# Cached attention in pairs of steps, with the transposes of its exponentials set apart

## The chip, the core and the metric

The program runs on one core of a Trainium2 chip. The metric is the device time of one launch in microseconds (us), as the median of several runs. Beside it stands one profiled execution, whose trace gives every number below that is not a run's time. The engines are TensorE (PE: matrix products; PEld: its weight loads), VectorE (DVE), ScalarE (ACT), GpSimd (POOL) and SyncE (SP, which here mostly issues loads). Each works through its own queue in order.

## The reference, cut to what matters

One step of a decoder layer over 512 prompt rows and 64 sample rows (8 sequences of 8 new positions). A projection gives queries, keys, values, forget-gate logits and the input of a convolution. Eight heads of 128 attend; the sample rows attend to 2048 cached positions, which a page table finds, and to the new ones. After it come the output projection, an MLP, a gated embedding and norms. The part that the change touches:

```python
def fox_attention_sample(q, k_new, v_new, logf_new, k_past, v_past, logf_past):
    ...
    s_past = jnp.einsum('bqhd,bkhd->bhqk', q, k_past).astype(jnp.float32) * scale
    s_past = s_past + cn[..., :, None] + r_past[..., None, :]
    ...
    p = jax.nn.softmax(jnp.concatenate([s_past, s_new], axis=-1), axis=-1).astype(v_new.dtype)
    return (jnp.einsum('bhqk,bkhd->bqhd', p[..., :P], v_past)
            + jnp.einsum('bhqk,bkhd->bqhd', p[..., P:], v_new))
```

## The kernel before

The program has two phases. The first, up to about 745 us, holds the input projection, both attentions and the convolution; the second the output projection, the MLP, the gate and the last norm. The order of work on every engine is written out by hand with Python generators: each `yield` ends a piece of work, and a loop decides whose piece comes next.

**The projection** sets the beat. A tile of 128 output columns (`gemm_tile`) takes four weight chunks of 256 KB; after each half of a chunk, 12 matmuls of 288 columns into bank U on L513, it yields. This piece is called a half tile here. Weights come through `WStream`: ACT issues the load (wraw, L117, five tiles in turn) and copies it to a rounded form (whi, L128), DVE makes the rest (wlo, L134), up to two chunks ahead of PE.

**Between two half tiles** `run` calls `half` once: first `flush_later`, which issues what was put off for a half tile (mostly exponentials, so that ACT does not wait in line for DVE), then one piece of the convolution, of the prompt heads (`att`) and of side work, and last, by a credit that grows by `DEC_RATE` (0.2275 to 0.2775), a step of cached attention, about one in four half tiles.

**Cached attention** (`decode`) has 68 steps. Four steps make a group: the 512 columns of one bank, for four sequences and four heads. A step n computes

- scores (up to n = 63), into bank D (`D_()`): at a group's first step one product that brings in the forget bias (R), then 8 products of 32 query columns with two k tiles. After the fourth step DVE adds a bias and takes the maximum (tile dp, in the source p); the exponential is put off to `later`, for ACT.
- values (from n = 4), for the group before, into bank O (`O_()`): 16 products of a 32-column piece of PT with two v tiles. PT holds the transposed exponentials of a group. After the fourth step DVE merges O into the running sum (`merge`).

The trace shows a product of these as two rows, 16 and 32 in a step. At the first step of a group, ahead of its scores, PE transposes the four blocks of the last group's exponentials into bank T (`T_()`, L869), and ACT copies them to PT in two pieces (L871). Bank T is also the prompt heads': their transposed exponentials, v_s (L798) and the end of each head, amt (L820), go through it. Each of the banks S, T, O and D has one buffer.

**The cache loads** (`kv_load`, L847) stand in SP's queue. A tile of keys or values is 512 KB in two loads; keys have five tiles, values four. A step's calls of `load` send, in this order, the second k tile and two v tiles for two steps later, and the first k tile for three steps later. A load waits for the products that read the tile's last content, and for the eighth load before it on the hardware queues, SP's and ACT's together, since eight completion semaphores are given out in turn.

Of the kernel before, what the change touches and what calls it, by code (L numbers as in the profile page):

```python
# [12 lines left out]
AF = mybir.ActivationFunctionType  # L13
# [134 lines left out]
class Kern:  # L148
# [111 lines left out]
    def phase1(self):  # L260
        tc, nc, a = self.tc, self.nc, self.a
# [108 lines left out]
        D = {"credit": 0.0, "dec": None, "mid": None, "rate": 0.0}  # L370

        def step(q):
            while q:
                try:
                    next(q[0])
                    return True
                except StopIteration:
                    q.popleft()
            return False

        def half():

            self.flush_later()
            if D["dec"] is None:
                step(att)
                step(fq)
                return
            step(side)
            step(att)
            step(pq)  # L390
            D["credit"] += D["rate"]
            if D["credit"] >= 1.0:
                D["credit"] -= 1.0
                if next(D["dec"], self) is self and D["mid"] is None:
                    des.close()
                    D["mid"] = mes.enter_context(tc.tile_pool(name="mid", bufs=2, reuse_waits="tile"))
                    self.ple_loads(D["mid"])
                    pq.append(self.ple_ahead(D["mid"]))
                    side.append(self.finish(1, D_, O_))

        def run(gen):
            for _ in gen:
                half()
# [41 lines left out]
        dec = D["dec"] = self.decode()  # L445
        next(dec)

        for n, (kind, i) in enumerate(order):
# [12 lines left out]
            if kind == "q":  # L461
                t = hd.tile([128, NR], F32, name="q", tag="q", bufs=2)
# [15 lines left out]
        n = 0  # L478
# [251 lines left out]

    def flush_later(self):

        for fn in self.later:
            fn()
        self.later = []


    def prompt_head(self, h, hb):
# [112 lines left out]
    def decode(self):  # L851


        nc, sm = self.nc, self.sm
        V = nc.vector.tensor_tensor
        tiles, load = self.kv, self.kv_load
        s = o = mu = p = None
        al, ls = {}, {}
        one = lambda name: sm.tile([128, 1], F32, name=name, tag=name)
        for n in range(68):  # L860
            if n == 0:
                load(0, 5)
                yield
            sc, w = n // 4, n % 4
            G, c = sc // 4, sc % 4
            if n >= 4 and w == 0:
                t = self.T_()
                for i in range(4):
                    nc.tensor.transpose(t[:, i * 128:i * 128 + 128], p[:, i * 128:i * 128 + 128], self.ident)  # L869
                for i, m in ((0, 128), (128, 512)):  # L870
                    nc.scalar.activation(self.PT[:, i:m], t[:, i:m], AF.Copy)  # L871
            if n < 64:
                if w == 0:
                    s = self.D_()
                    nc.tensor.matmul(s, self.selU[:, G, :], self.R[:, c * 512:c * 512 + 512], start=True, stop=False)
                for i in range(2):
                    kt = tiles[0][2 * n + i]
                    for h in range(4):
                        nc.tensor.matmul(s[32 * h:32 * h + 32, i * 256:i * 256 + 256].rearrange("p (a b) -> p a b", a=2),  # L879
                                         self.q_of(G // 2 * 4 + h, G % 2 * 4 + w), kt[:, :, h, :],  # L880
                                         start=False, stop=(w == 3 and i == 1))
                if w == 3:
                    p = self.kvp[1].tile([128, 512], F32, name="dp", tag="dp")
                    mx = one("dmx")
                    nc.vector.tensor_scalar(p, s, self.cns[:, G:G + 1], None, ALU.add, ALU.max, accum_out=mx)
                    new = self.mlu[:, 0, G:G + 1]
                    if c == 0:
                        nc.vector.tensor_copy(new, mx)
                        ls[sc] = self.mlu[:, 1, G:G + 1]
                    else:  # L890
                        al[sc], ls[sc] = one("dal"), one("dls")
                        V(mx, mx, new, ALU.max)
                        V(al[sc], new, mx, ALU.subtract)
                        nc.vector.tensor_copy(new, mx)
                    nm = one("dnm")
                    nc.vector.tensor_scalar(nm, mx, -1.0, None, ALU.mult)

                    def late(p=p, nm=nm, l=ls[sc], d=al.get(sc)):
                        nc.scalar.activation(p, p, AF.Exp, bias=nm, accum_out=l)
                        if d is not None:  # L900
                            nc.scalar.activation(d, d, AF.Exp)
                    self.later.append(late)
                load(0, 2 * n + 6)
            if n >= 4:
                m = n - 4
                if w == 0:
                    o = self.O_()
                for r in range(4):
                    for h in range(4):
                        nc.tensor.matmul(o[32 * h:32 * h + 32, r * 128:r * 128 + 128], self.PT[:, w * 128 + h * 32:w * 128 + h * 32 + 32],  # L910
                                         tiles[1][2 * m + r // 2][:, r % 2, h, :], start=(w == 0 and r == 0), stop=(w == 3 and r == 3))
                if w == 3:
                    self.merge(m // 16, m // 4 % 4, o, al.pop(m // 4, None), ls.pop(m // 4))
            load(1, 2 * n - 2)
            load(0, 2 * n + 7)
            yield

    def merge(self, G, c, o, al, l):

# [881 lines left out]
class Beside:  # L1801
# [41 lines left out]
    def wait(self, t, dt):  # L1843
        self.now = t
        self.credit = min(max(self.credit, -3.0) + dt, dt)
# [173 lines left out]
```

## Time and profile before

| what | value |
|---|---|
| median of 3 runs | 2682.98 us (2680.68 to 2690.61) |
| the profiled execution's own time | 2673.58 us |
| its span, first to last instruction | 2671.5 us |
| granted TensorE clock | 0.997 |
| PE / DVE / ACT / POOL busy, share of the span | 98% / 77% / 44% / 20% |
| score products (L879), count and mean | 1024, 385 ns |
| value products (L910), count and mean | 2048, 273 ns |
| transposes of exponentials (L869), count and mean | 64, 274 ns |

The profile's page gives busy time by engine, the span in 40 slices of 67 us, the chain of work that ended last, and groups of instructions. Matmuls overlap on PE, so a sum of their durations is more than the time that they take; what a burst costs is read from starts, in the view in order of time. There, a row with a count merges like instructions that follow each other, with the start of the first and the time to the end of the last.

### The profile page before, as it was taken

What the parts mean: (1) busy time and instruction counts of PE and PEld (TensorE: products, weight loads), DVE (VectorE), ACT (ScalarE), POOL (GpSimd) and SP (SyncE); (2) the same over time, 40 slices, a digit from 0 to 9 for tenths busy, and PEclk for the clock granted to TensorE, in tenths of its full rate; (3) what the DMA queues carried; (4) which work ended last, traced back from release to release, by engine and by line L of the source; (5) the groups of instructions that cost most, each with busy time, mean ns of one, the idle gap of its engine ahead of it and who ended that gap; (6) DMA issues with size and microseconds to landing.
All of it is one profiled execution on the core that took longest, in us unless ns stands there. A gap on an engine that the chain in (4) does not pass through costs nothing.

```text
span 2671.5 us, 56560 instructions
## 1 busy us (share of the span) xinstructions
PE 2631.2 (98%) x21937; PEld 2555.2 (96%) x21937; DVE 2050.0 (77%) x3575; ACT 1164.8 (44%) x1722; POOL 521.0 (20%) x919
## 2 busy tenths in 40 slices
PE   9999999999999999999999999999999999999997
PEld 8899999888999999999999999999999999999997
DVE  6577777656564348888998888899888888898676
ACT  5222223335453335444544444545444444444554
POOL 2288786711010000000100000110000000000110
PEclk9999999999999999999999999999999999999998
DMA  6598999899764554444444444767565666656675
GB/s 206 172 305 292 300 297 303 291 319 319 270 200 148 164 195 157 156 143 157 168 163 143 144 145 143 253 184 219 154 199 137 174 173 175 174 187 217 196 241 169
DMA packets 241327, 544.39 MB, mean 204 GB/s; under 512 B 25921, under 2 KB 26946, under 8 KB 241058
## 3 DMA queue, kind: packets, MB, share of 16 engines
q1 hardware_dynamic: 172562, 330.95, 38.6%
q0 software_dynamic: 34960, 148.86, 17.7%
q10 hardware_dynamic: 33536, 60.96, 7.1%
q8 instruction: 172, 2.82, 0.4%
q14 instruction: 97, 0.79, 0.1%
HBM read 445.60 MB, written 95.09 MB: 202 GB/s over the span
## 4 chain that ended last, share of the span: by engine, by line
PE 85%; issue 5%; DVE 5%; DMA 3%; ACT 1%; POOL 0%; SPq 0%; ACTq 0%; DVEq 0%; POOLq 0%
PE U L513 20%; PE P L1661 17%; PE P L1662 16%; PE P L1663 16%; PE P L1731 2%; PE P L1730 2%; PE P L1729 2%; PE D L879 2%; PE O L910 2%; DVE w2l L157 1%; DMA wraw<-in_w_main 1%; DMA xs<-dl 1%; PE S L753 1%; PE S L773 1%; DMA w2r<-in_w_down 0%
## 5 line engine op out<-in xcount | busy, mean ns | idle before, releaser
L1661 PE MATMUL P<-xs,w2h 128*128 128x288 f32 x3584 | 1061.5, 296 | 5.2 <-DVE c L1778 4.7
L1662 PE MATMUL P<-xs,w2h 128*128 128x288 f32 x3584 | 1056.7, 295 | 3.2 <-DVE xs L157 2.8
L1663 PE MATMUL P<-xs,w2l 128*128 128x288 f32 x3584 | 1051.5, 293 | 0.6 <-DVE w2l L157 0.5
L154 ACT ACTIVATE w2h<-w2r 128x896 fp32r<-128x896 f32 (+1 forms) x632 | 558.9, 890 | 758.9 <-PE P L1662 439.4
L157 DVE TENSOR_TENSOR w2l<-w2r,w2h 128x896 fp32r<-128x896 f32 (+1 forms) x632 | 637.9, 1012 | 197.5 <-ACT w2h L154 191.7
L1661 PEld LDWEIGHTS P<-xs,w2h 128*128 128x128 f32 x3584 | 672.7, 188 | 9.6 <-DVE c L1778 6.7
L1662 PEld LDWEIGHTS P<-xs,w2h 128*128 128x128 f32 x3584 | 675.0, 188 | 5.1 <-DVE xs L157 4.3
L1663 PEld LDWEIGHTS P<-xs,w2l 128*128 128x128 f32 x3584 | 675.0, 188 | 1.5 <-DVE w2l L157 1.5
L513 PE MATMUL U<-xh,whi 128*128 128x288 f32 x1792 | 399.3, 304 | 0.4 <-ACT xh L154 0.4
L513 PE MATMUL U<-xl,whi 128*128 128x288 f32 x1792 | 383.1, 295 | 1.8 <-DVE xl L348 0.9
L513 PE MATMUL U<-xh,wlo 128*128 128x288 f32 x1792 | 383.5, 296 | 0.0
L513 PEld LDWEIGHTS U<-xh,whi 128*128 128x128 f32 x1792 | 286.8, 189 | 19.0 <-issue 16.3
L128 ACT ACTIVATE whi<-wraw 128x512 fp32r<-128x512 f32 x224 | 140.9, 630 | 354.6 <-PE U L513 323.8
L513 PEld LDWEIGHTS U<-xl,whi 128*128 128x128 f32 x1792 | 288.0, 188 | 2.8 <-DVE xl L348 1.4
L513 PEld LDWEIGHTS U<-xh,wlo 128*128 128x128 f32 x1792 | 287.9, 188 | 0.0
L134 DVE TENSOR_TENSOR wlo<-wraw,whi 128x512 fp32r<-128x512 f32 x224 | 159.8, 714 | 118.3 <-ACT whi L128 117.9
L1059 DVE SCALAR_TENSOR_TENSOR y<-ue,cv,y 128x512 f32<-128x512 f32 x240 | 183.7, 765 | 5.3
L1884 DVE TENSOR_TENSOR w2r<-w2r 128x512 f32<-128x512 f32 (+1 forms) x273 | 177.9, 652 | 10.9 <-DMA w2r<-in_w_down 10.7
L1060 POOL TENSOR_SCALAR cvt<-us,cv 128x64 f32<-128x64 f32 x240 | 165.8, 691 | 22.3
L1731 PE MATMUL P<-xs,w2l 128*128 128x288 f32 x512 | 151.0, 295 | 1.1 <-DVE w2l L157 1.0
L1730 PE MATMUL P<-xs,w2h 128*128 128x288 f32 x512 | 150.9, 295 | 0.8 <-DVE xs L1570 0.8
L1729 PE MATMUL P<-xs,w2h 128*128 128x288 f32 x512 | 151.3, 295 | 0.0
(413 smaller groups left out, 2795.2 us busy)
## 6 DMA issues: line engine op xcount, KB each, us to landing
k<-in_cache_kv SPq DMA_DIRECT2D x256, 256.0 KB, 4.3
v<-in_cache_kv SPq DMA_DIRECT2D x256, 256.0 KB, 4.5
w2r<-in_w_up SPq DMA_DIRECT2D x127, 512.0 KB, 3.9
w2r<-in_w_down SPq DMA_DIRECT2D x112, 512.0 KB, 4.3
wraw<-in_w_main ACTq DMA_DIRECT2D x156, 256.0 KB, 4.7
xs<-di POOLq DMA_DIRECT2D x32, 1008.0 KB, 6.2
w2r<-in_w_gate SPq DMA_DIRECT2D x60, 512.0 KB, 4.8
x<-c POOLq DMA_DIRECT2D x48, 576.0 KB, 5.8
```

Of the source, the lines that this page charges most:

```text
L154: self.nc.scalar.activation(out, in_, AF.Copy, **kw)
L157: self.nc.vector.tensor_tensor(out, in_, f(hi), ALU.subtract)
L513: self.nc.tensor.matmul(u[:, r, :HR], w, x[:, r * HR:(r + 1) * HR], start=first and n == 0, stop=last and n == 2)
L1059: nc.vector.scalar_tensor_tensor(y, ue[:, j:j + NPR], w, y, ALU.mult, ALU.add)
L1060: nc.gpsimd.tensor_scalar(t, us[:, :, j:j + 8], w, None, ALU.mult)
L1661: nc.tensor.matmul(o, hi[:, ia, :], s.hi[:, ib, :], start=(i == 0), stop=False)
L1662: nc.tensor.matmul(o, hi[:, ia, :], s.lo[:, ib, :], start=False, stop=False)
L1663: nc.tensor.matmul(o, lo[:, ia, :], s.hi[:, ib, :], start=False, stop=(i == n - 1))
L1729: nc.tensor.matmul(o, hi[:, ia, :], s.hi[:, kh, rows], start=first and kh == 0, stop=False)
L1730: nc.tensor.matmul(o, hi[:, ia, :], s.lo[:, kh, rows], start=False, stop=False)
L1731: nc.tensor.matmul(o, lo[:, ia, :], s.hi[:, kh, rows], start=False, stop=last and kh == 1)
L1884: lambda: V(w[:, :, 4:6, :], w[:, :, 0:1, :].broadcast_to([128, m, 2, 128]), w[:, :, 1:3, :], ALU.add),
```

## The change

Three things are different.

1. `half` waits until the credit is 2 and then takes two steps of cached attention one after the other. The rate is the same, so two steps stand in one burst every seven to nine half tiles. As step numbers go in pairs from 0, a group's steps are two bursts: first and second, third and fourth. The last step no longer yields, so that the second call of the last pair reports the end.
2. The transposes leave the first step of the next group. They are a function `turn` that is put into `later` by a new helper `wait`, which hands it on through three flushes: the exponential is issued one half tile after the group's last scores, the transposes three half tiles after that. They go to bank D, the score bank, and ACT copies all 512 columns to PT in one instruction. A loop at a group's first step flushes until its transposes are done, if they aren't yet.
3. `flush_later` takes the list away before it calls its entries, so that an entry may put off another.

```diff
-            if D["credit"] >= 1.0:
-                D["credit"] -= 1.0
-                if next(D["dec"], self) is self and D["mid"] is None:
+            if D["credit"] >= 2.0:
+                D["credit"] -= 2.0
+                if [next(D["dec"], self) for _ in range(2)][1] is self and D["mid"] is None:
...
-        for fn in self.later:
+        fns, self.later = self.later, []
+        for fn in fns:
             fn()
-        self.later = []
+
+    def wait(self, k, fn):
+
+        self.later.append((lambda: self.wait(k - 1, fn)) if k else fn)
...
-            if n >= 4 and w == 0:
-                t = self.T_()
-                for i in range(4):
-                    nc.tensor.transpose(t[:, i * 128:i * 128 + 128], p[:, i * 128:i * 128 + 128], self.ident)
-                for i, m in ((0, 128), (128, 512)):
-                    nc.scalar.activation(self.PT[:, i:m], t[:, i:m], AF.Copy)
+            while n >= 4 and w == 0 and turned[0] < sc:
+                self.flush_later()
...
-                    def late(p=p, nm=nm, l=ls[sc], d=al.get(sc)):
+                    def turn(p=p):
+                        t = self.D_()
+                        for i in range(4):
+                            nc.tensor.transpose(t[:, i * 128:i * 128 + 128], p[:, i * 128:i * 128 + 128], self.ident)
+                        nc.scalar.activation(self.PT, t, AF.Copy)
+                        turned[0] += 1
+
+                    def late(p=p, nm=nm, l=ls[sc], d=al.get(sc), turn=turn):
                         nc.scalar.activation(p, p, AF.Exp, bias=nm, accum_out=l)
                         if d is not None:
                             nc.scalar.activation(d, d, AF.Exp)
+                        self.wait(2, turn)
...
-            yield
+            if n < 67:
+                yield
```

The next two pieces are the difference on PE, at the start of the third group (- before, + changed). At the place where a burst with the transposes stood, half a pair after the second group's last scores:

```order
 L513 MATMUL U<-xh_209,wlo 128x288 x2
-L869 MATMUL T<-ident,dp 128x128 x4
-L875 MATMUL D<-R,selU 128x512
-L879 MATMUL D<-k,q_s 32x256 x8
-L910 MATMUL O<-v,PT 32x128 x16
+L902 MATMUL D<-ident,dp 128x128 x4
 L513 MATMUL U<-xh_195,whi 128x288 x2
```

The transposes stay there alone, in bank D, and the step has moved down. Next on PE, where the group's second step stood:

```order
 L513 MATMUL U<-xh_201,wlo 128x288 x2
-L879 MATMUL D<-k,q_s 32x256 x8
-L910 MATMUL O<-v,PT 32x128 x16
+L876 MATMUL D<-R,selU 128x512
+L880 MATMUL D<-k,q_s 32x256 x8
+L919 MATMUL O<-v,PT 32x128 x16
+L880 MATMUL D<-k,q_s 32x256 x8
+L919 MATMUL O<-v,PT 32x128 x16
 L513 MATMUL U<-xh_203,whi 128x288 x2
```

Both steps now stand there, without projection between them. On ACT the copies to PT keep their place among the weight chunks. Before:

```order
L899 ACTIVATE dp,dls<-dp,dnm 128x512
L901 ACTIVATE dal<-dal 128x1
L117 DMA wraw<-in_w_main 128x512
L128 ACTIVATE whi<-wraw 128x512
L117 DMA wraw<-in_w_main 128x512
L128 ACTIVATE whi<-wraw 128x512
L871 ACTIVATE PT<-T 128x128
L871 ACTIVATE PT<-T 128x384
```

Changed:

```order
L907 ACTIVATE dp,dls<-dp,dnm 128x512
L909 ACTIVATE dal<-dal 128x1
L117 DMA wraw<-in_w_main 128x512
L128 ACTIVATE whi<-wraw 128x512
L117 DMA wraw<-in_w_main 128x512
L128 ACTIVATE whi<-wraw 128x512
L903 ACTIVATE PT<-D 128x512
```

Two chunks lie between the exponential and the copy in both; the copy is one instruction. SP's queue holds the same loads in the same order; of each load only the product that it waits for stands in another place.

More of the change, by code (lines that the diff above doesn't have):

```diff
@@ L858, in decode @@
         al, ls = {}, {}
+        turned = [0]
         one = lambda name: sm.tile([128, 1], F32, name=name, tag=name)
```

## Prediction

> **What bounds the kernel now.** I read the page first, then the stretch in which cached attention runs, then single bursts in the order of time, then the loads.
>
> ```profile
> span 2671.5 us, 56560 instructions
> PE 2631.2 (98%) x21937; PEld 2555.2 (96%) x21937; DVE 2050.0 (77%) x3575; ACT 1164.8 (44%) x1722; POOL 521.0 (20%) x919
> ...
> DMA  6598999899764554444444444767565666656675
> ```
>
> TensorE is busy from end to end, so every microsecond that it loses or wins moves the end. The row of DMA digits shows a second load: slices 3 to 11, 67 us each, stand at eight or nine tenths, which is where keys and values of the cache stream in. The score products (bank D) and the value products (bank O) by source line, with shortest, median and longest duration in ns and first and last start in us:
>
> ```profile
> L879 PE MATMUL D<-k,q_s x1024: 376/379/404, 97.6 to 700.4; 128*32 128x256 f32 x171
> L910 PE MATMUL O<-v,PT x2048: 272/273/297, 131.1 to 738.2; 128*32 128x128 f32 x187
> ```
>
> From the first of the 64 score steps to the last are 700.4 - 97.6 = 602.8 us, 9.57 us from one to the next (63 intervals); two steps take 19.1 us. The stretch as a whole, by the view of windows (busy time and count of PE, PEld, DVE, ACT, POOL; clock; DMA share; GB/s):
>
> ```profile
> 97.00:745.00 648.00, 641.48 (x6922) 582.93 (x6921) 432.17 (x903) 215.37 (x458) 343.89 (x616) 1.00 0.87 290
> 650.00:700.00 50.00, 50.00 (x600) 44.95 (x602) 30.44 (x89) 29.54 (x62) 6.67 (x13) 1.00 0.96 344
> ```
>
> PE is busy for 641 of 648 us, at full clock. DMA moves 290 GB/s at 87%, and at one place it kept up 344 GB/s at 96% with PE still fully busy. So the change is worth what it takes off PE's queue here, less what later loads put back.
>
> **One burst, and what joining two saves.** An ordinary step (not the first of its four), as PE ran it:
>
> ```profile
> 139.93 0.42 PE L513 MATMUL U<-xh,wlo 128*128 128x288 f32 x2
> 140.28 1.07 PE L879 MATMUL D<-k,q_s 128*32 128x256 f32 x16
> 141.17 1.06 PE L910 MATMUL O<-v,PT 128*32 128x128 f32 x32
> 142.15 0.53 PE L513 MATMUL U<-xh,whi 128*128 128x288 f32 x2
> 142.52 0.42 PE L513 MATMUL U<-xl,whi 128*128 128x288 f32 x2
> ```
>
> Undisturbed pairs of L513 start 0.265 us apart. From the last pair before the burst to the second after it are 142.52 - 139.93 = 2.59 us; less two times 0.265 the step costs 2.06 us. Of this, 0.28 us are its edges:
> - entry: 140.28 - 139.93 = 0.355, 0.09 over an undisturbed pair;
> - exit: 32 value products stream for 1.06 - 0.27 + 0.11 = 0.90 us (the last start, and the four-product beat of 0.11 behind it), but 0.98 pass until L513 is back: 0.08;
> - the first pair after it takes 142.52 - 142.15 = 0.37: 0.105 over.
>
> Between D and O there is no edge: 0.89 us is what 16 score products stream (1.07 - 0.385, and one beat of 0.215).
>
> Two steps in one burst drop one exit and one entry, 0.28 us, and put a change from O to D in their place, which no row shows. Its bounds: nothing (as D to O, same shape 128*32) and all of 0.28 (as any entry, which then saves nothing). I take 0.03, by the nearest row, D to O, with a little for the waits on two landed k tiles that stand at its head: 0.25 saved. 68 steps become 34 bursts; I count 32 joins, since some steps stand next to a prompt head's burst today and share an edge with it already: **32 x 0.25 = 8.0 us saved**, between 0 and 9.0.
>
> The Trainium skill, page "TensorEngine Tiling (Array Packing)", Tiling Modes, Key Properties, says that changing the tiling mode drains TensorE while changing only the tile does not. By it O to D costs nothing, the join saves 32 x 0.28 = 9.0, and the forecast would be 1 us lower. The trace agrees at D to O; it has no row of O to D.
>
> **The transposes on their own.** Before, they stand at the head of every fourth burst, into bank T, with the copy to PT and then the value products behind them. Now they stand four half tiles after the scores' end, in bank D, and interrupt the projection by themselves. The first rows are the old place, the others show another group of four transposes that stands alone today:
>
> ```profile
> 129.47 0.60 PE L869 MATMUL T<-ident,dp 128*128 128x128 f32 x4
> 129.82 0.47 PE L875 MATMUL D<-R,selU 128*128 128x512 f32 x1
> ...
> 409.52 0.43 PE L513 MATMUL U<-xh,wlo 128*128 128x288 f32 x2
> 409.79 0.60 PE L765 MATMUL T<-ident,p 128*128 128x128 f32 x4
> 410.14 0.51 PE L513 MATMUL U<-xh,whi 128*128 128x288 f32 x2
> 410.49 0.42 PE L513 MATMUL U<-xl,whi 128*128 128x288 f32 x2
> ```
>
> In the burst they take 0.35 us; alone 410.49 - 409.79 - 0.265 = 0.435. Sixteen groups: **16 x 0.085 = 1.4 us lost**. Bank D is then free, since the maximum that reads it comes before the exponential that the transposes need, and the next group's scores come about five half tiles after the copy. ACT does one copy of 512 columns in place of two of 128 and 384; it is busy for 215 of 648 us in this stretch, so I cost that at nothing.
>
> What the old place cost in waits is in the list of waits and at the worst burst:
>
> ```profile
> PEld O L910 <- ACT PT L871: 1.4, 2, 0.8
> PEld T L869 <- ACT amt L822: 1.3, 1, 1.3
> PEld T L869 <- ACT v_s L799: 1.0, 1, 1.0
> ...
> 586.05 0.42 PE L513 MATMUL U<-xh,wlo 128*128 128x288 f32 x2
> 587.50 0.66 PE L869 MATMUL T<-ident,dp 128*128 128x128 f32 x4 [1.03 <-ACT amt L822]
> 588.33 1.07 PE L879 MATMUL D<-k,q_s 128*32 128x256 f32 x16
> 589.73 1.08 PE L910 MATMUL O<-v,PT 128*32 128x128 f32 x32 [0.33 <-ACT PT L871]
> ```
>
> Bank T is shared with the prompt heads (amt, v_s), and the value products wait for PT. Both waits go: the bank is another, and PT is copied half a pair ahead. **1.4 + 1.3 + 1.0 = 3.7 us saved** (0 if the transposes wait for a late exponential instead, which is what is late next on ACT).
>
> **The loads.** Keys have five tiles, values four; a step reads two of each and frees them, and SP sends the next loads in the order k, v, v, k. A pair now reads four and four, eight tiles of nine. The loads of its first step can go out only one step later than before. What hides that is the lateness that SP has already. Tiles freed by the value products at 391.63 get their loads at 401.93, and are read at 413.46:
>
> ```profile
> 391.63 1.06 PE L910 MATMUL O<-v,PT 128*32 128x128 f32 x32
> 401.93 3.15 SPq L847 DMA_DIRECT2D v<-in_cache_kv  x4
> 411.75 2.90 SPq L847 DMA_DIRECT2D v<-in_cache_kv  x4
> 413.46 1.06 PE L910 MATMUL O<-v,PT 128*32 128x128 f32 x32
> DMA to landing us min/median/max: 2.6/4.5/8.2
> ...
> SPq L847 <- PE D L879: 35.7, 12, 8.3
> ...
> SPq L847 <- DMA wraw<-in_w_main: 23.0, 14, 3.3
> ```
>
> The load goes out 10.3 us after the reading began, about one step. SP isn't waiting for PE there: the last two rows are SP's waits in 97 to 200 us, for PE, and in 200 to 300 us, for landings of weight loads (loads of SP and ACT take eight completion semaphores in turn, so each waits for the eighth before it). So a tile freed one step later is freed about when its load goes out today. At the median landing of 4.5 us the tiles arrive at 405.1 + 4.5 = 409.6, 3.9 us before they are read, and the pair's second value products are read 2.06 us later still. I put **2 us lost** on the whole stretch for late v tiles. From below: 0. From above: a pair's chain on SP is 0.9 us to the first freeing, 14 issues up to the last v at (2.90 - 0.33)/3 = 0.86 us, 12.0 us, waits for weights of 23% of 19.1 us, 4.4 us, and a landing of 4.5 to 8.2: 21.8 to 25.5 us. It may take 19.1 + 2.06 + 0.89 = 22.05. At the median it just fits, at the longest landing it is 3.5 us late.
>
> **The sum.** -8.0 + 1.4 - 3.7 + 2 = -8.3 us. Against the profiled execution's own 2673.58 us (span 2671.5, and 2.1 around it) this gives 2665.3. The runs' median is 2682.98, 9.4 us higher, from 2680.68 to 2690.61; I carry the difference over: **2675 us**. What stands outside the stretch is as before. Half a percent (13.4 us) is about what a measurement here can tell from no change.
>
> **Rivals.**
> - *The loads become the bound* (slower). A pair takes eight of nine tiles, so DMA and SP rest at each burst and PE then waits inside the next one for v. For it: DMA at 96% in one window, SP's chain fits at the median landing only. Against it: 344 GB/s was sustained, and SP is a step late today without harm. Halfway between on time and 3.5 us late is 1.75 us; in the 26 pairs from 200 to 700 us, 45 us; less the 10.3 us saved, 2683 + 35 = 2718 us. It outweighs the saving from 0.4 us per pair on. The Trainium skill, page "DMA: Bandwidth & Descriptors", Issuing engines are not separate DMA queues, speaks for this rival: loads issued by SP and ACT run on the same 16 engines and interleave, so bunched k and v loads would also delay the weights. SP's waits for weight landings agree with it; no row shows PE waiting for them.
> - *The join saves nothing*, O to D costing as much as an exit and an entry. For it: the waits on k tiles stand at the head of each D. Against it: D to O is free. 1.4 - 3.7 + 2 = -0.3: 2683 us.
> - *All of it counts*: 9.0 by the join, 3.7, no late tiles, and the waits for v of today gone too. PE's own waits are 6.5 us in the whole stretch (648 - 641.48), 3.7 of them counted above, so at most 2.8 more: -9.0 + 1.4 - 3.7 - 2.8 = -14: 2669 us.
>
> **How the numbers follow.** The forecast, from -11 to -3, has 0.47; all of it counts 0.20; the join saves nothing 0.15; the loads bound 0.18. The forecast's own range is 2670 to 2681. The medians of few runs move by some 5 us (before: 2680.68 to 2690.61), so 2669 becomes 2663 at its low end, and of the rival of loads the milder half, up to +19 us, is taken in: 2663 to 2702. Faster by over 0.5% (below 2669.6) has half of "all of it", 0.10, and by the runs' own spread some of the others, 0.13: 0.23. Slower (above 2696.4) has the greater part of the loads' rival, 0.15, and 0.05 for what I don't see: 0.20. Within 0.5%: 0.57.
>
> **What would show it.** Right: joined bursts of about 2 x 2.06 - 0.25 = 3.87 us between pairs of L513; transposes alone at some 0.43 us; no wait of the value products on PT nor of transposes on amt or v_s; SP waiting little for PE after 200 us. Wrong: value or score products that wait for landings of v or k inside the second half of a burst by over 0.4 us on average; SP's waits for PE of several us per pair; L513 waiting for whi behind a late weight load; transposes that wait for the exponential.

## The result and the profile after

The changed kernel is slower, by little: 2687.62 us median (2679.24 to 2695.79, 22 runs) against 2679.84 us (2672.08 to 2690.61, 22 runs) for the kernel before in the same sessions. The ratio is 1.0021, 95% interval 1.0011 to 1.0031. The first four lines are from the page of the changed kernel; the fifth and sixth, by source line, are its score and value products and answer to those of L879 and L910 before; the last two are from its view of windows, the whole stretch and one place in it (busy time and count of PE, PEld, DVE, ACT, POOL; clock; DMA share; GB/s).

```profile
span 2685.4 us, 56526 instructions
PE 2631.2 (98%) x21937; PEld 2561.8 (95%) x21937; DVE 2049.2 (76%) x3575; ACT 1163.3 (43%) x1706; POOL 522.2 (19%) x919
DMA  6588898998865454444544444777565665656675
PE 78%; DMA 8%; issue 6%; DVE 5%; ACT 1%; SPq 0%; POOL 0%; ACTq 0%; DVEq 0%; POOLq 0%
...
L880 PE MATMUL D<-k,q_s x1024: 379/379/404, 104.3 to 712.0; 128*32 128x256 f32 x171
L919 PE MATMUL O<-v,PT x2048: 272/273/423, 138.7 to 748.6; 128*32 128x128 f32 x187
...
97.00:745.00 648.00, 628.57 (x6801) 578.61 (x6799) 427.29 (x888) 209.80 (x430) 347.39 (x620) 0.99 0.87 291
605.00:610.00 5.00, 4.57 (x24) 4.19 (x25) 0.00 (x0) 0.00 (x0) 0.00 (x0) 0.50 0.99 358
```

In the stretch of cached attention PE is busy for 628.6 of 648 us where it was 641.5: it now idles 19.4 us there in place of 6.5. The fourth line is the chain of work that ended last, and it has 8% of DMA where it was 3% before; the longest value product is 423 ns, where the longest before was 297. Transfers move as many bytes per microsecond as before (291 GB/s against 290).

What PE waits for in this stretch (list of waits: total us, times, longest):

```profile
PE O L919 <- DMA v<-in_cache_kv: 14.4, 17, 2.1
PE T L769 <- ACT p L763: 2.7, 1, 2.7
...
PEld O L919 <- DMA v<-in_cache_kv: 21.0, 22, 2.4
```

No wait for PT and none of the transposes for amt or v_s is left. In their place the value products wait for v tiles. Step by step (first start to last start of a step's 32 value products, over the median step's 0.78 us) they lose 18.6 us in the changed kernel, 18.5 of it in the second step of a pair. In the kernel before, the same reading gives 1.6 us.

An undisturbed burst, one with a late tile, and the worst one, in the order of time:

```profile
155.67 0.43 PE L513 MATMUL U<-xh,wlo 128*128 128x288 f32 x2
156.03 1.07 PE L880 MATMUL D<-k,q_s 128*32 128x256 f32 x16
156.91 1.06 PE L919 MATMUL O<-v,PT 128*32 128x128 f32 x32
157.79 1.05 PE L880 MATMUL D<-k,q_s 128*32 128x256 f32 x16
158.65 1.06 PE L919 MATMUL O<-v,PT 128*32 128x128 f32 x32
159.64 0.53 PE L513 MATMUL U<-xh,whi 128*128 128x288 f32 x2
160.01 0.42 PE L513 MATMUL U<-xl,whi 128*128 128x288 f32 x2
...
442.94 1.05 PE L880 MATMUL D<-k,q_s 128*32 128x256 f32 x16
443.80 0.91 PE L919 MATMUL O<-v,PT 128*32 128x128 f32 x24
446.52 0.42 PE L919 MATMUL O<-v,PT 128*32 128x128 f32 x8 [1.81 <-DMA v<-in_cache_kv]
446.88 0.53 PE L513 MATMUL U<-xh,whi 128*128 128x288 f32 x2
...
603.92 0.65 PE L919 MATMUL O<-v,PT 128*32 128x128 f32 x8 [2.13 <-DMA v<-in_cache_kv]
605.43 0.66 PE L919 MATMUL O<-v,PT 128*32 128x128 f32 x8 [0.85 <-DMA v<-in_cache_kv]
606.01 0.85 PE L513 MATMUL U<-xh,whi 128*128 128x288 f32 x2
606.66 0.69 PE L513 MATMUL U<-xl,whi 128*128 128x288 f32 x2
607.14 0.69 PE L513 MATMUL U<-xh,wlo 128*128 128x288 f32 x2
```

The first burst costs 160.01 - 155.67 - 0.53 = 3.81 us. In the second the last quarter of the value products waits for the last half of the last v tile. In the third the second and third of its waits are shown (the first, of 0.95 us, ended at 601.37), and behind them pairs of L513 start 0.48 us apart in place of 0.265: the clock is granted at half, as the window 605 to 610 says (0.50).

SP's loads in the pair before the second of these, and its waits from 200 to 700 us; the last line is the same wait in the kernel before:

```profile
425.96 3.69 SPq L851 DMA_DIRECT2D v<-in_cache_kv  x4
430.16 6.19 SPq L851 DMA_DIRECT2D k<-in_cache_kv  x4
436.91 3.75 SPq L851 DMA_DIRECT2D v<-in_cache_kv  x4
...
SPq L851 <- DMA wraw<-in_w_main: 91.6, 44, 4.8
SPq L851 <- PE D L880: 23.8, 7, 9.9
...
SPq L847 <- DMA wraw<-in_w_main: 102.9, 56, 4.5
```

The four value loads that began at 436.91 are the last that this burst needs; the last of them goes out at 440.33 (the row's end less 0.33 for one issue), and its bytes are there at 446.5, 2 us after PE asks for them. SP has hardly a pause in this round: from 423 to 441 us its waits are 5.3 us together, 2.2 of them for PE, and the rest of the time it issues loads. It had hardly one in the kernel before either: from 200 to 700 us its waits for PE were 12 us there, those for landings 115.

### The profile page after: what moved, and what is told of

It is laid out like the page before. It is cut to its first block, busy times and chain, and to the rows that moved or that the text cites. A ratio compares the mean times of both kernels' runs of the same rounds, so it can differ in the third digit from the quotient of the medians.

```text
span 2685.4 us, 56526 instructions
## 1 busy us (share of the span) xinstructions
PE 2631.2 (98%) x21937; PEld 2561.8 (95%) x21937; DVE 2049.2 (76%) x3575; ACT 1163.3 (43%) x1706; POOL 522.2 (19%) x919
## 4 chain that ended last, share of the span: by engine, by line
PE 78%; DMA 8%; issue 6%; DVE 5%; ACT 1%; SPq 0%; POOL 0%; ACTq 0%; DVEq 0%; POOLq 0%
PE U L513 17%; PE P L1671 16%; PE P L1672 16%; PE P L1673 16%; PE P L1741 2%; PE P L1740 2%; PE P L1739 2%; DMA v<-in_cache_kv 2%; DMA wraw<-in_w_main 2%; PE O L919 1%; PE D L880 1%; DVE w2l L157 1%; DMA w2r<-in_w_down 1%; DMA xs<-dl 1%; PE S L757 1%
## 5 line engine op out<-in xcount | busy, mean ns | idle before, releaser
L154 ACT ACTIVATE w2h<-w2r 128x896 fp32r<-128x896 f32 (+1 forms) x632 | 558.8, 890 | 760.3 <-PE P L1672 429.9
L513 PE MATMUL U<-xh,whi 128*128 128x288 f32 x1792 | 400.5, 305 | 0.0
L513 PE MATMUL U<-xl,whi 128*128 128x288 f32 x1792 | 385.0, 296 | 1.9 <-DVE xl L348 1.0
L513 PE MATMUL U<-xh,wlo 128*128 128x288 f32 x1792 | 385.1, 297 | 0.0
L513 PEld LDWEIGHTS U<-xh,whi 128*128 128x128 f32 x1792 | 289.3, 190 | 12.6 <-issue 10.5
L513 PEld LDWEIGHTS U<-xl,whi 128*128 128x128 f32 x1792 | 289.7, 190 | 3.3 <-DVE xl L348 1.9
L513 PEld LDWEIGHTS U<-xh,wlo 128*128 128x128 f32 x1792 | 289.5, 189 | 0.0
```

The costliest lines, as they stand in the source:

```text
L154: self.nc.scalar.activation(out, in_, AF.Copy, **kw)
L513: self.nc.tensor.matmul(u[:, r, :HR], w, x[:, r * HR:(r + 1) * HR], start=first and n == 0, stop=last and n == 2)
```

## The experiments

Ratios are to the kernel before, in the same session. "Late v" and "late k" are the time lost between first and last start of a step's value or score products, as above. They are read from one profiled execution of each kernel; those of 2 and 3 were 5 and 10 us faster than the median of their runs, that of 5 was 9 us slower, so a difference of a few us in late tiles between two runs says little. In the code cuts, ... stands for what is left out.

**1. The transposes alone.** Single steps again; the transposes apart, in bank D, one flush sooner.

```diff
-            if D["credit"] >= 2.0:
-                D["credit"] -= 2.0
-                if [next(D["dec"], self) for _ in range(2)][1] is self and D["mid"] is None:
+            if D["credit"] >= 1.0:
+                D["credit"] -= 1.0
+                if next(D["dec"], self) is self and D["mid"] is None:
...
-                        self.wait(2, turn)
+                        self.wait(1, turn)
```

> One part alone: single steps as before, the transposes on their own in the score bank (three half tiles after the scores, not four, since single steps follow each other closer). Theory A (the loss comes from the second step's v tiles, which a pair reads too soon for their place in SP's queue): no pair, so no late v; the waits on PT and bank T go (3.7 us) and the lone transposes cost 1.4, so 2 us faster than before, ratio 0.998 to 1.000. Theory C (the transposes' new place costs): 3 to 6 us slower than before, with PE waiting for the exponential or bank D.

Measured: 2682.02 us, ratio 1.0009 [0.9989, 1.0030]; late v 5.1 us. The transposes alone don't move the time measurably. Late v, which I had expected to stay away without pairs, is 3.5 us more than before, about what the transposes were to win.

**2. The pairs alone.** The kernel before with two steps per burst; the transposes stay in the burst, through bank T.

```diff
-            if D["credit"] >= 1.0:
-                D["credit"] -= 1.0
-                if next(D["dec"], self) is self and D["mid"] is None:
+            if D["credit"] >= 2.0:
+                D["credit"] -= 2.0
+                if [next(D["dec"], self) for _ in range(2)][1] is self and D["mid"] is None:
...
-            yield
+            if n < 67:
+                yield
```

> The other part alone: steps in pairs, the transposes at the head of the group's first step through bank T as before. Theory A: late v tiles in the second step of a pair as in the changed kernel, 15 to 20 us of waits inside its value products, and half clock after the longest; the joins save 8; so 4 to 10 us slower than before, ratio 1.002 to 1.004. Theory C: pairs are then harmless and it is faster than before by 5 to 8 us.

Measured: 2687.32 us, ratio 1.0020 [1.0003, 1.0037]; late v 9.6 us, 9.5 of it in second steps. The loss comes with the pairs; the late tiles are fewer than the 15 to 20 us that I expected.

**3. A fifth value tile, one key tile less.**

```diff
-    KVA, KVN = 3, (5, 4)
+    KVA, KVN = 3, (4, 5)
...
-                load(0, 5)
+                load(0, 4)
...
-            load(1, 2 * n - 2)
-            load(0, 2 * n + 7)
+            load(1, 2 * n - 1)
```

> The changed kernel with one tile moved from keys to values (four k tiles, five v tiles, same memory); k tiles are then loaded right behind the scores that free them. Theory A: one v tile of the second step is loaded a pair earlier, the waits in the second step's value products fall from 18.6 us to under 5, no half clock; 8 to 12 us faster than before, ratio 0.995 to 0.997. Theory B (bunched loads as a whole are more than DMA can bring): the wait moves to k or to the first step, time as the changed kernel or worse, ratio 1.002 or more.

Measured: 2691.57 us, ratio 1.0037 [1.0017, 1.0057]; late v 9.5, late k 4.2 us, all in second steps. What v won, k lost in part, and the runs are no faster: the split of nine tiles between keys and values isn't at fault. More tiles in all were not tried.

**4. The last value tile's loads ahead of the second key tiles'.**

```diff
-                load(0, 2 * n + 6)
+                if n % 2 == 0:
+                    load(0, 2 * n + 6)
...
-            load(0, 2 * n + 7)
+            if n % 2:
+                load(0, 2 * n + 7)
```

> The changed kernel with the order of SP's loads alone changed: in the second step of a pair the three k tiles are sent behind the two v tiles instead of around them. Nothing else differs. Theory A: the second step's v loads go out four issues (3.5 us) earlier, k tiles had 12 us to spare; waits in the second step's value products fall from 18.6 us to under 4, no half clock; 8 to 12 us faster than before, ratio 0.995 to 0.997. Theory B: k tiles are late instead, time as the changed kernel, ratio 1.001 to 1.003.

Measured: 2689.32 us, ratio 1.0036 [1.0016, 1.0056]; late v 1.2, late k 13.7 us. What PE waits for now, in the list of waits from 97 to 745 us:

```profile
PE D L880 <- DMA k<-in_cache_kv: 13.9, 17, 2.7
```

Seventeen waits again, with the other name. The order of the loads decides who is late, not whether somebody is: the round of 16 loads as a whole takes too long. The theory that the order was at fault fell here.

**5 and 6. Half as many cache loads**, on the changed kernel and, as a base, on the kernel before. Both halves of a tile come by one load of 512 KB, from the first of its two pages; every second page is not read.

```diff
-            for x in range(2):
-                b, pg = (w, 2 * j + x) if i == 0 else (2 * j + x, w)
...
+            b, pg = (w, 2 * j) if i == 0 else (2 * j, w)
...
+            nc.sync.dma_start(t.rearrange("p x h c -> p x (h c)"),
+                              a["cache_kv"][bass.ds(r, 1), G // 2 * 2 + i].rearrange("o p c -> p o c").broadcast_to([128, 2, 512]))
```

> The changed kernel with one load of 512 KB for a tile in place of two of 256 KB. Part of the computation is left out for it: both halves of a tile are read from the first of its two pages, so every second page of the cache is not read (as many bytes move as before). Theory A2 (late tiles come from SP's queue: 16 issues a pair at 0.86 us, and waits on a ring of eight semaphores that it shares with the weights): half the issues and twice the bytes in the ring, so the waits in a pair's second step fall from 18.6 us to under 4; 8 to 12 us faster than the kernel before, ratio 0.995 to 0.997. Theory B (DMA's throughput right behind a burst, whatever the queue): waits stay at 10 to 20 us, ratio 1.001 to 1.004.

> The kernel before (single steps, transposes in the burst) with the same joined loads and the same part left out: what these do without pairs. Both theories: there were 1.6 us of waits in the value products, so 0 to 3 us faster, ratio 0.998 to 1.001. The difference to the paired kernel with joined loads is then what pairs and transposes give when tiles are in time: 8 to 11 us by the working of the prediction.

Measured: with pairs 2664.45 us, ratio 0.9923 [0.9904, 0.9942], late v 0.1 and late k 0.3 us; with single steps 2679.74 us, ratio 0.9977 [0.9964, 0.9990]. By the medians (6 runs of the first, 12 of the second) the pairs and the transposes are worth 2679.74 - 2664.45 = 15.3 us when tiles are in time; run 8 gives a narrower reading, 11.7 us. The stretch with pairs by the view of windows, and SP's waits from 200 to 700 us:

```profile
97.00:745.00 648.00, 642.53 (x7084) 597.79 (x7084) 437.15 (x928) 220.26 (x459) 345.71 (x622) 1.00 0.83 295
...
SPq L850 <- PE D L879: 182.0, 37, 12.4
SPq L850 <- DMA k<-in_cache_kv: 49.7, 23, 4.5
SPq L850 <- DMA wraw<-in_w_main: 24.8, 9, 4.3
```

SP now waits for PE, 182 us of 500: it is ahead. PE is busy 642.5 us and the clock is full; bytes per microsecond are those of the others. A load takes longer to land here, 7.7 us for v at the median where it is 4.5 in the changed kernel, and yet no tile is late.

**7. The value loads on POOL's queue.**

```diff
+            q = nc.gpsimd if i else nc.sync
...
-                r = nc.sync.value_load(self.pti[0:1, e:e + 1])
-                nc.sync.dma_start(t[:, x].rearrange("p h c -> p (h c)"),
+                r = q.value_load(self.pti[0:1, e:e + 1])
+                q.dma_start(t[:, x].rearrange("p h c -> p (h c)"),
```

> The changed kernel, nothing left out, with the loads of v tiles issued by POOL in place of SP: other completion semaphores, and SP's queue holds the k loads alone. Theory A2: waits in the second step fall under 5 us; 4 to 10 us faster than the kernel before, ratio 0.996 to 0.999, if POOL's own loads and convolution products don't come late behind waiting v loads. Theory B: waits of 10 us or more stay, ratio 1.001 to 1.004.

Measured: 2805.7 us, ratio 1.0438 [1.0420, 1.0455]. PE's waits and the stretch:

```profile
PE O L920 <- DMA v<-in_cache_kv: 59.7, 62, 2.9
PE U L513 <- DVE wlo L134: 18.5, 4, 7.7
...
97.00:745.00 648.00, 564.10 (x5658) 500.19 (x5658) 362.38 (x702) 157.04 (x311) 412.47 (x800) 0.93 0.73 241
```

My expectation failed: tiles come later still. On POOL the work stands in one order, and the convolution's stands between the loads: behind a v load at 308.04 us POOL multiplies for the convolution and waits 4.1 us for the landing of a load of its own (st), and the next v load goes out at 323.73.

**8. The kernel before once more**, for one profile.

> The kernel before, unchanged, for a second trace: the first one's execution, 2673.6 us, was among the fastest of its runs, whose median is 2681. All theories: its span is 2674 to 2683 us; if the clock is halved for some us in it without pairs, such stretches aren't due to the change alone.

Measured: span 2686.1 us, above what I expected; late v 1.9 us, and the clock is halved nowhere between 97 and 745 us. The MLP's first product (bank P) starts 3.0 us later than in the profile shown before the change, and the rest of the 14.6 us lies behind it. So spans of single profiles aren't compared here: the MLP and what follows, which the change doesn't touch, vary by more than the change is worth.

The part with cached attention is steadier. From the last product ahead of it (S<-cs,LD, at 89.05 us in the first profile) to the end of the last value product are 649.4 us in the first profile of before and 649.8 in the second. The other traces, read the same way:

| run | us | late v + late k |
|---|---|---|
| the changed kernel | 659.6 | 18.6 |
| 1, transposes alone | 650.6 | 5.1 |
| 2, pairs alone | 652.0 | 9.9 |
| 3, a fifth value tile | 649.9 | 13.7 |
| 4, v loads ahead of k | 657.2 | 14.9 |
| 5, joined loads, pairs | 636.1 | 0.4 |
| 6, joined loads, single steps | 647.7 | 0.2 |
| 7, value loads on POOL | 773.9 | 74.4 |
| 9, two loads of one page | 657.2 | 16.4 |
| 10, half of the weight loads | 640.9 | 3.8 |
| 11, second value tiles by ACT | 686.6 | 1.8 |
| 12, paired weight loads, pairs | 662.0 | 20.8 |
| 13, paired weight loads, single steps | 658.1 | 6.6 |

The changed kernel loses 10.0 us here (659.6 against 649.6), and with joined loads the pairs and the transposes win 11.7 us (run 5 against run 6). Run 3 doesn't fit: its trace has late tiles and no loss, and its execution was 10 us faster than the median of its runs. What made up for the late tiles there is open.

**9. Two loads per tile, both from its first page.** Every second page is not read, as in 5, but the number of loads is that of the changed kernel.

```diff
-                b, pg = (w, 2 * j + x) if i == 0 else (2 * j + x, w)
+                b, pg = (w, 2 * j) if i == 0 else (2 * j, w)
```

> The changed kernel with two loads per tile as it has, but both of them from the tile's first page, so that every second page of the cache is not read (as in the run with joined loads, whose 16 loads per pair were 8). Theory A, the number of loads that SP has to put out (16 per pair, each with its own issue and its own wait for a turn) makes the tiles late, and where the bytes lie has no part in it: value products of second steps still lose 12 to 20 us, ratio 1.000 to 1.004. Rival B, the run with joined loads was fast because the same page is read twice and so comes sooner: second steps lose under 3 us, ratio 0.990 to 0.996.

Measured: 2686.77 us, ratio 1.0017 [1.0002, 1.0032]; late v 16.4 us, 16.3 of it in second steps.

```profile
PE O L919 <- DMA v<-in_cache_kv: 11.7, 16, 1.9
```

That both halves come from the same page has no part in it. The rival fell; what helped in 5 is that there are half as many loads, each twice as large.

**10. Half of the weight loads.** A weight chunk with odd number uses the weights of the one before it.

```diff
-    AHEAD, RAW, TILES = 2, 4, 5
+    AHEAD, RAW, TILES = 2, 4, 3
...
-            self.raw[self.sent] = t
-            self.sent += 1
+            self.raw[self.sent] = self.raw[self.sent + 1] = t
+            self.sent += 2
```

> The changed kernel with every second load of a weight chunk left out (a chunk uses the weights of the one before it; half of the weights of the input and output projections are not read). SP's own work per cache load stays as it is. Theory A1, SP loses its time in the waits for a completion semaphore that a weight load still holds (92 us in 44 waits between 200 and 700 us): these waits fall under 50 us, the value products of second steps lose under 6 us, ratio 0.992 to 0.998. Theory A2, SP's issue alone (16 loads of about 0.86 us of 22) fills the pair: second steps still lose over 10 us, ratio 0.999 to 1.003.

Measured: 2672.86 us, ratio 0.9945 [0.9919, 0.9970]; late v 3.3 us. SP's waits for weight landings from 200 to 700 us are 67.5 us in 34 waits, not under 50, so the theory had the time right, and the mark it had set in SP's waits was missed. The output projection also reads half of its weights here, but the gain doesn't come from it: the last value product ends 9.2 us earlier than in the kernel before, the MLP's first product behind the output projection starts 9.3 us earlier.

**11. The second step's value tiles loaded by ACT**, two half tiles (one weight chunk) after the burst; SP has 12 loads in a pair.

```diff
-    def kv_load(self, i, m):
+    def kv_load(self, i, m, eng=None):
...
-            load(1, 2 * n - 2)
+            if n % 2:
+                self.wait(1, lambda n=n: load(1, 2 * n - 2, nc.scalar))
+            else:
+                load(1, 2 * n - 2)
```

> The changed kernel with the value tiles of a pair's second step loaded by ACT, one chunk of the projection after the burst; SP has 12 loads per pair where it had 16, and all pages are read. Theory A, SP's chain of loads is what is late: the second steps lose under 6 us, and where ACT's rounding of the weights keeps its lead the ratio is 0.993 to 0.999. Rival, four loads of about 0.9 us and their waits in ACT's order make the rounded weights late: PE waits for weights over 10 us between 97 and 745 us, ratio over 1.003.

Measured: 2719.58 us, ratio 1.0125 [1.0103, 1.0147]. Late v is 0.8, late k 1.0 us: SP's chain was the trouble. But ACT stands still for its loads, and what waits is its rounding of the weights:

```profile
ACT whi L128 <- PE U L513: 82.7, 29, 8.7
ACT whi L128 <- DMA v<-in_cache_kv: 77.8, 20, 11.4
```

ACT's waits for PE cost nothing, since it is ahead there; those 77.8 us for v are new. The rival was right that ACT's other work would be late, but only in part where I had looked: PE's waits for weights are 6.5 us, not over 10, those of the prompt heads' transposes for ACT's exponentials 12.3 us.

**12 and 13. Weight loads in pairs of chunks**, 512 KB each, all bytes read; on the changed kernel and on the kernel before. To make room the low parts have two buffers in place of three.

```diff
-            t = self.pool.tile([128, 4, 128], F32, name="wraw", tag="wraw", bufs=self.TILES)
-            (self.nc.sync if self.sent < self.RAW else self.nc.scalar).dma_start(t, self.srcs[self.sent])
-            self.raw[self.sent] = t
-            self.sent += 1
+            t = self.pool.tile([128, 2, 4, 128], F32, name="wraw", tag="wraw", bufs=3)
+            (self.nc.sync if self.sent < self.RAW else self.nc.scalar).dma_start(t, self.srcs[self.sent // 2])
+            self.raw[self.sent], self.raw[self.sent + 1] = t[:, 0], t[:, 1]
+            self.sent += 2
...
```

> The changed kernel with the projections' weights loaded two chunks at a time (512 KB per load in place of two of 256 KB, three such buffers; to make room two buffers of the low parts in place of three, made once per chunk), all bytes read. Theory A1, the late tiles come from the number of loads that take turns at the completion semaphores: second steps lose under 6 us, ratio 0.993 to 0.999, less what the shorter lead of the low parts costs (PE's waits for the low parts, 0 to 5 us). Rival B, the bytes that the run with half of the weight loads left out are what counted there: second steps lose 10 us or more, ratio 1.000 to 1.006.

> The kernel before with the same paired weight loads: single steps, transposes in the burst. It is the base for the run above. Theory A1: its value tiles are in time already (1.4 us lost before), so the paired loads bring it only what the low parts cost, ratio 0.998 to 1.004, and the paired kernel beats it by 6 to 15 us. Rival B: the two differ by under 4 us.

Measured: with pairs 2690.78 us, ratio 1.0032 [1.0016, 1.0048]; with single steps 2687.0 us, ratio 1.0013 [0.9998, 1.0028]; late v 20.1 and 6.3 us. The first of them still waits, and so does SP:

```profile
PE O L917 <- DMA v<-in_cache_kv: 14.8, 22, 2.0
...
SPq L849 <- DMA wraw<-in_w_main: 94.1, 33, 5.7
```

Fewer turns at the completion semaphores don't help when each weight load is twice as long: 33 waits of 2.9 us on the mean in place of 44 of 2.1. Theory A1, as I had written it, fell. So one thing lengthens SP's round by these runs for sure, the number of cache loads (5 against 9, at equal bytes). The weights' loads lengthen it too (10); that it is their bytes and not their number is suggested by 10 against 12, at equal numbers of weight loads, but not shown: the edit of 12 and 13 has a price of its own, since its base with single steps is 8.5 us longer in the table above.

How large the parts are can be read: in a pair of the changed kernel, 19.6 us on the mean, 16 issues at 0.86 us take 13.8 us, and the waits for landings, 105 of 500 us, take 4.1. What each would bring alone isn't separated. No version that reads everything beat the kernel before.

## Why the prediction failed, step by step

*The joins: right, a little better.* 3.81 us per undisturbed joined burst against 3.87 forecast; 32 times (2 x 2.06 - 3.81) is 9.9 us in place of 8.0, and above the 9.0 that I had called the most. From O to D there is no edge (157.79 - 156.91 = 0.88, as D to O), where I had taken off 0.03. The Trainium skill's page "TensorEngine Tiling (Array Packing)", Tiling Modes, Key Properties, says that a change of the tiling mode drains TensorE and a change of the tile alone does not; O and D have one shape, 128*32, and the trace agrees. The rival "the join saves nothing" is out.

*The transposes and their waits: right.* In the order of time of the changed kernel:

```profile
165.86 0.43 PE L513 MATMUL U<-xh,wlo 128*128 128x288 f32 x2
166.13 0.60 PE L902 MATMUL D<-ident,dp 128*128 128x128 f32 x4
166.48 0.52 PE L513 MATMUL U<-xh,whi 128*128 128x288 f32 x2
166.84 0.43 PE L513 MATMUL U<-xl,whi 128*128 128x288 f32 x2
```

They cost 166.84 - 166.13 - 0.265 = 0.445 us, forecast 0.435. The waits for PT and bank T are gone. The 3.7 us for them came from the list of PEld; PE's own list before has 1.0 + 0.7 + 0.7 = 2.4 us, so the term was between 2.4 and 3.7.

*The loads: here it failed*, at the sentence that a tile freed one step later is freed about when its load goes out today, so that SP's lateness hides the later freeing; hence "2 us lost". The lost time is 18.6 us against 1.6 before, 17.0 more. What happened is in the lead: the time from the last v load of a step going out to the step's first value product (means of the 42 to 44 steps that start between 200 and 620 us, read from the starts of the rows):

| lead of the last v load, us | first step of a pair | second step | median landing of v |
|---|---|---|---|
| before (the same steps, single) | 8.3 | 7.3 | 4.5 |
| before, second profile (8) | 8.1 | 7.4 | 4.5 |
| changed | 12.9 | 4.2 | 4.5 |
| changed, joined loads (5) | 17.1 | 14.3 | 7.7 |

The first step's tiles gained 4.6 us and the second's lost 3.1, and 14 of the 21 second steps were left with a lead under 4.5 us, a median landing. At the median the landings are no longer than before. Of the ten steps that lost over 0.3 us, eight had a lead of 0.8 to 4.3 us; the two at 558.8 and 600.0 us, with leads of 6.2 and 4.2 us, had landings of 8.8 us and more. With joined loads the landings are longer, the leads too, and nothing is late.

Two readings hid this. The rows at 391.63, 401.93 and 413.46 belong to steps that become the first of a pair, the ones that gain; the second step's loads stand in the next row (411.75, the last out at 414.3), and I held no read against them. And the lead of 8.7 us in those rows was taken for all: over the stretch it was 2.2 to 14.4 us. The upper bound in the same part had the mechanism: SP's round of 21.8 to 25.5 us against 22.05 allowed. I took its middle landing and called it fitting, which left 0.25 us for everything else.

The rival "the loads become the bound" was the right mechanism with too high a price: 1.75 us per pair there, 18.5 / 32 = 0.58 measured. That is above its point of decision, 0.4.

*What I didn't see, two smaller terms.* One wait of the prompt heads' transposes for the exponential p, 2.7 us at one place, where the list of before has two, 1.2 us together; such a wait of 2 us or more stands in every kernel with pairs, and what makes p late there I don't know. And the clock: after waits for v at 252 and 600 to 604 and after that wait for p at 645 it was granted at half for 3.4, 6.8 and 3.4 us, which costs half of that, at most 6.8 us.

The sum with these: -9.9 + 1.4 - 3.7 + 17.0 + 1.5 = +6.3 us, and up to 6.8 more by the clock. The part with cached attention is 10.0 us longer in the trace, between the two; the medians' ratio gives 3 to 8 us. So the sign turned on one term. The time came out inside the range, 5 us above its middle, but only because the range had taken in the milder half of the loads' rival; the forecast's own mechanism ended at 2681.

The gain is there, as the joined loads show (11.7 us by the traces, against 9.9 - 1.4 + 3.7 - 1.5 = 10.7 by the terms), and it's taken back by v.

## What to carry to other kernels

Work that is put together on the bounding engine also puts its reads together, while the queue that loads for it goes on sending one load after the other: the first reads of a burst gain lead and the last ones lose it. So check the last tile of the burst, not any tile, and over the whole stretch: set its lead, from its load going out to its read, against the landing. Where the issuing queue has no pause in the old profile (hardly a wait for the reader, only issues and waits for landings), assume that it hides nothing. If a wait only changes its name when loads are reordered or buffers moved, it's the round that is too long. Fewer, larger loads helped here, though only in a run that leaves out half of the pages; another engine's queue helps only if nothing that the bound needs stands in it.

## What the runs showed of the hardware

The clock halves after shorter waits than I had thought worth a term. Rows of the changed kernel by the view of windows:

```profile
255.00:260.00 5.00, 5.00 (x27) 5.00 (x28) 0.35 (x1) 0.35 (x1) 4.09 (x11) 0.66 0.91 316
600.00:605.00 5.00, 1.49 (x28) 0.48 (x20) 2.19 (x4) 0.68 (x1) 0.54 (x1) 0.86 1.04 391
645.00:650.00 5.00, 2.28 (x9) 2.00 (x9) 4.72 (x10) 3.64 (x7) 2.14 (x4) 0.80 0.59 172
```

PE's wait ahead of the first half clock is 1.85 us and ahead of the last 2.7; ahead of the second stand two, 0.95 and 2.13 us. The half clock lasts 3.4 us or twice that. Other steps that lost as much (at 291 and at 444, 2.3 and 2.1 us, the first in two waits) had none behind them. The Trainium skill's page "TensorE: Matmul & The Clock Gate", What's actually happening, gives an idle window of about 3.4 us, free-running, as what takes the clock down; the durations agree with it, but the waits here are shorter than one window, alone or, at 600, with a short burst between them, so by these rows less than a whole idle window can be enough.

The half clock makes late loads cost more than their waits: with the value loads on POOL, 59.7 us of waits of the value products stand beside a clock of 0.93 over the whole stretch.
